# A weight sum moved from VectorE to an accumulating transfer, in four pairs of a feed-forward stage

## The chip, the cores and the metric

The kernel runs on one core of one Trainium2 chip. The metric is the device time of one execution in microseconds (us), as the median of several runs. A core has TensorE for matrix products (PE in the profile; its weight loads are PEld), VectorE (DVE), ScalarE (ACT), GpSimd (POOL) and SyncE (SP). In this kernel SP and POOL do hardly anything but issue transfers. Each engine works through its own queue in order, and waits on semaphores for the others.

## The reference

Two layers work on 512 rows of 1024 numbers in float32: an attention or mLSTM mixer, a cross-attention to a memory of 256 rows, and a feed-forward part with a short causal convolution. Only the last is touched:

```python
def conv_ffn(xn, w_up, conv_w, conv_b, w_down):
    h = causal_depthwise_conv(xn @ w_up, conv_w) + conv_b
    g, u = jnp.split(h, 2, axis=-1)
    return (jax.nn.gelu(g) * u) @ w_down
```

`w_up` is 1024 x 5632 and `w_down` 2816 x 1024.

## The kernel before

Everything is kept transposed: channels on the 128 partitions, the 512 rows along the free axis. The 5632 columns of `w_up` are handled as 22 pairs of 128-wide blocks; pair p holds block p of the half g and block p of the half u. Float32 accuracy comes from splitting each operand into a high and a low part in a faster format (`wh` and `wl`, `xh` and `xl`) and making three matrix products of them: lines L291, L292, L293 in `mm3`. The high part is a cast on ScalarE (L1747, or L285 and L1554 elsewhere), the low part a difference on VectorE (L282).

Pair 0 is done plainly (`plain`). Pairs 1 to 21 go through `seven`, a Strassen-Winograd product: the 2 x 2 blocks (two halves of the weights' rows, g and u; two halves of the input, two halves of the 512 rows) are multiplied with seven products instead of eight. That takes sums of the weights ahead of it, which for each pair are made anew:

- S1 (tile `sa`, 1024 wide): one load on SP, and one accumulating transfer on POOL which adds the other block to it on the way (`onto`, L1732).
- S2 (tile `sb`, 512 wide): the right half of S1 plus the left half of the block A1 (tile `raw`), on VectorE, L1753.
- S4: S2 plus the right half of A1, in place in `sb`, on VectorE, L1759.
- each of S1, S2, S4, A1 and a piece of the other block (`ra`) is then split into high and low.

The products are p1 to p7 in the code. p1 and p2 fill one accumulator (X), p6, p7 and p4 a second (Y), p5 and p3 a third (R). Between them ScalarE copies a state of Y or R away: L1786 (`seed`, Y starts as minus X after p1), L1790 (`kept`: `u5` after p5 from R, `u2` after p6 from Y), and L1793 on VectorE subtracts these. So p6 waits for L1786, p7 for `u2`, p3 for `u5`, and p4 for the L1793 that reads Y. L1816 scales the result by the norm, and `tail` makes the convolution (L1669 on ScalarE, four taps L1676 on VectorE), the gelu (L1684), the product with u (L1686) and its split (`ah`, L1690).

The order of work on each engine is not the order in the code. `add`, `load`, `onto` and `pe` only record tasks for a planner (`Sched`), each with an engine, an assumed duration, what it depends on, a due time, and the buffers it takes and gives back. The planner goes through the tasks engine by engine, always taking the one which could start first, on equal starts the one with the earlier due time; from that follow the queues. A task that is added, removed or given other durations can thus move others. Buffers: `raw` and `sa` have three, `sb` and `ra` two. A buffer of `sb` is taken at S2's making and given back after S4 is split.

Of the kernel before, what the change touches and what calls it, by code (L numbers as in the profile page):

```python
# [65 lines left out]
class Plan:  # L66
# [11 lines left out]
    def add(self, fn, dur=0.0, deps=(), prio=None, take=(), free=(), chain=(), pre=(), after=0.0, order=(), load=(), st=None):  # L78
        it = Item(fn, dur, [d for d in deps if d is not None], len(self.items) if prio is None else prio, take, free, chain, pre, after, order, load, st)
        it.n = len(self.items)  # L80
        self.items.append(it)
        return it
# [154 lines left out]
class Builder:  # L237
# [1269 lines left out]
    def ffn_steps(self, layer, mp):  # L1507
# [5 lines left out]
        add = sc.add  # L1513
        tt = lambda n: 0.055 + 1.06e-3 * n
# [17 lines left out]
        def raw_tile(st, tag):  # L1532
            pool, n, bufs = RAWS[tag]
            st[tag] = self.til(pool, tag, (P, n), bufs=bufs)
            return st[tag]

        def load(st, tag, src, cols, at, dur=0.0017):
            def fn():
                to = raw_tile(st, tag)[:, :cols]
                nc.sync.dma_start(to.rearrange("p (a b) -> p a b", a=2) if len(src.shape) == 3 else to, src)  # L1540

            return add("SP", dur * cols, fn, (), at, [(tag, st)], (), 4.0)

        def parts(st, off=0):
            st["wh"], st["wl"] = self.parts(off)
# [177 lines left out]
        def seven(p, fill):  # L1723
            st, sa, sb, r2, f1, f3, s2, s4, a22 = ({} for _ in range(9))
            at = clock[0]
            A1, A2 = t["up"][layer, p], t["up"][layer, 22 + p]
# [4 lines left out]
            def onto(out, src, cols, deps, due):  # L1731
                return add("POOL", 0.0029 * cols, lambda: nc.gpsimd.dma_start(out(), src(), accum_op=ALU.add), deps, due, (), (), 6.0)  # L1732
# [3 lines left out]
            b1 = load(sa, "sa", up2[p][:, :, :512], 1024, at - 20.0 - soon, 0.0 if soon else 0.0017)  # L1736
            b1 = onto(lambda: sa["sa"][:], lambda: A2, 1024, [b1], at - 16.0 - soon)
            l2 = load(r2, "raw", A1, 1024, at - 12.0)
# [5 lines left out]
            def split(s, cols, deps, due, alloc, take, raw, free=()):  # L1744
                def hi():
                    alloc()
                    nc.scalar.copy(s["wh"][:, :cols], raw())  # L1747

                h = add("ACT", act(cols), hi, deps, due - 3.0, take)
                return add("DVE", tt(cols), lambda: self.sub(s["wl"][:, :cols], raw(), s["wh"][:, :cols]), [h], due - 2.0, (), free)  # L1750
# [1 line left out]
            def s2_():  # L1752
                tt_(out=raw_tile(sb, "sb")[:], in0=sa["sa"][:, 512:], in1=r2["raw"][:, :512], op=ALU.add)  # L1753

            b2 = add("DVE", tt(512), s2_, [b1, l2], at - 5.0, [("sb", sb)])
            w3 = split(f3, 1024, [l2], at, lambda: parts(f3, OFF), [("h", f3)], lambda: r2["raw"][:])
            w2 = split(s2, 512, [b2], at, lambda: small(s2, "s2"), [("s2", s2)], SB)
            w1 = split(f1, 1024, [b1], at + 1.0, lambda: parts(f1, OFF), [("h", f1)], lambda: sa["sa"][:])
# [537 lines left out]
```

## Time and profile before

| | us |
|---|---|
| median of 3 runs (1458.19 to 1459.31) | 1459.03 |
| the profiled execution | 1458.72 |
| its span, first to last instruction | 1456.9 |
| first sum L1753 in layer 0 / in layer 1 | 405.4 / 1108.7 |

The feed-forward stage of layer 0 begins near 406 us and that of layer 1 near 1109 us. In the profile's rows a name like `acc<-xh,wh` is output and inputs by the program's tile names; the first number is the start in us from the span's start, the second the duration, and brackets hold the idle time of that engine ahead of the row and whoever ended it. A duration includes the pipeline's fill, so on a busy engine the distance of two starts is the better price. PE's ends are modelled.

### The profile page before, as it was taken

To read this page: it belongs to the slowest core of one execution; us is meant where nothing else is said; L and a number is where in the kernel's file an instruction comes from. 1 tells how busy PE (TensorE), PEld (TensorE's weight loads), DVE (VectorE), ACT (ScalarE), POOL (GpSimd) and SP (SyncE) were. 2 spreads that over 40 slices of the span, in tenths; PEclk is the share of its full clock that TensorE was granted. 3 is DMA by queue.
4 is the path that set the end of the run, shared out by engine and by line. 5 is a ranking of instruction groups with operands and counts; after the bars stand their busy time and mean duration, and the time that the engine had idled before them with its cause. 6 is when DMAs were issued, how large, how long until landed. Compare 5 with 4: busy or idle time off the path is not lost.

```text
span 1456.9 us, 24068 instructions
## 1 busy us (share of the span) xinstructions
PE 1440.6 (99%) x9019; PEld 1277.7 (88%) x9019; DVE 1225.9 (84%) x2224; ACT 985.5 (68%) x1775; POOL 72.9 (5%) x116
## 2 busy tenths in 40 slices
PE   9999999999999999999999999999999999999998
PEld 7888787998899999999888888889988999999987
DVE  7789987867899988889669988887779998888974
ACT  7689665655677777777547665566566777777764
POOL 0001120000000000000000100000000000000000
PEclk9999999999999999999999999999999999999999
DMA  5222436652246656662233332656413666656322
GB/s 200 87 74 73 118 122 195 169 179 87 94 122 169 183 158 157 155 160 77 84 101 108 111 109 65 204 142 189 131 49 117 162 178 173 154 157 160 104 67 78
DMA packets 70628, 190.24 MB, mean 131 GB/s; under 512 B 7520, under 2 KB 7520, under 8 KB 70512
## 3 DMA queue, kind: packets, MB, share of 16 engines
q1 hardware_dynamic: 62304, 161.38, 35.0%
q0 software_dynamic: 7200, 26.22, 10.6%
q8 instruction: 70, 1.15, 0.3%
q10 hardware_dynamic: 1008, 1.12, 0.2%
q14 instruction: 46, 0.38, 0.1%
HBM read 186.56 MB, written 2.13 MB: 130 GB/s over the span
## 4 chain that ended last, share of the span: by engine, by line
PE 82%; DVE 10%; ACT 4%; issue 2%; DMA 2%; SPq 0%; POOL 0%; ACTq 0%; DVEq 0%; POOLq 0%
PE acc L291 15%; PE acc L292 14%; PE acc L293 14%; PE w L293 6%; PE w L291 6%; PE w L292 6%; PE s L293 3%; PE s L291 3%; PE s L292 3%; PE acc L352 2%; PE acc L354 2%; PE acc L353 2%; DVE wl L282 2%; DMA sa<-in_xq_dram 1%; DVE x L771 1%
## 5 line engine op out<-in xcount | busy, mean ns | idle before, releaser
L282 DVE TENSOR_TENSOR wl<-raw,wh 128x1024 fp32r<-128x1024 f32 (+3 forms) x181 | 213.9, 1182 | 41.2 <-ACT wh L285 32.4
L291 PE MATMUL acc<-xh,wh 128*128 128x256 f32 (+1 forms) x624 | 206.8, 331 | 0.2 <-ACT v L1917 0.2
L293 PE MATMUL acc<-xh,wl 128*128 128x256 f32 (+1 forms) x624 | 205.6, 329 | 0.1
L292 PE MATMUL acc<-xl,wh 128*128 128x256 f32 (+1 forms) x624 | 205.5, 329 | 0.0
L285 ACT CAST wh<-raw 128x1024 fp32r<-128x1024 f32 (+1 forms) x123 | 126.6, 1034 | 84.3 <-PE acc L292 42.9
L1676 DVE SCALAR_TENSOR_TENSOR c<-hs,vec,c 128x512 f32<-128x512 f32 x176 | 130.4, 749 | 16.0 <-ACT c L1669 14.0
L291 PEld LDWEIGHTS acc<-xh,wh 128*128 128x128 f32 x624 | 117.2, 188 | 12.1 <-ACT v L1917 0.6
L293 PEld LDWEIGHTS acc<-xh,wl 128*128 128x128 f32 x624 | 117.2, 188 | 12.0 <-DVE wl L282 0.5
L292 PEld LDWEIGHTS acc<-xl,wh 128*128 128x128 f32 x624 | 117.2, 188 | 11.5
L293 PE MATMUL w<-ah,wl 128*128 128x512 f32 x304 | 119.1, 392 | 0.0
L292 PE MATMUL w<-al,wh 128*128 128x512 f32 x304 | 118.6, 390 | 0.0
L291 PE MATMUL w<-ah,wh 128*128 128x512 f32 x304 | 118.5, 390 | 0.0
L282 DVE TENSOR_TENSOR wl<-sa,wh 128x1024 fp32r<-128x1024 f32 x52 | 63.6, 1222 | 17.0 <-ACT wh L1747 15.6
L1669 ACT ACTIVATE c<-hs,vec 128x512 f32<-128x512 f32 x88 | 71.2, 816 | 9.6 <-DVE hs L1816 8.2
L1747 ACT CAST wh<-sa 128x1024 fp32r<-128x1024 f32 x42 | 44.0, 1049 | 35.5 <-PE w L292 30.5
L293 PEld LDWEIGHTS w<-ah,wl 128*128 128x128 f32 x304 | 57.1, 188 | 12.1
L291 PEld LDWEIGHTS w<-ah,wh 128*128 128x128 f32 x304 | 57.1, 188 | 10.1 <-ACT w L1584 0.2
L292 PEld LDWEIGHTS w<-al,wh 128*128 128x128 f32 x304 | 57.1, 188 | 9.8
L282 DVE TENSOR_TENSOR s<-sb,s 128x512 fp32r<-128x512 f32 x92 | 63.1, 686 | 2.2 <-ACT s L285 0.3
L1554 ACT CAST wh<-dr 128x512 fp32r<-128x512 f32 x64 | 39.7, 621 | 34.2 <-PE w L292 32.2
L1732 POOL DMA_DIRECT2D sa<-in_up_dram x42 | 35.9, 855 | 516.5 <-DVE wl L282 184.5
L291 PE MATMUL acc<-mem,wh 128*128 128x256 f32 (+1 forms) x192 | 61.5, 320 | 0.0
(535 smaller groups left out, 4664.1 us busy)
## 6 DMA issues: line engine op xcount, KB each, us to landing
raw<-in_up_dram SPq DMA_DIRECT2D x46, 512.0 KB, 3.4
sa<-in_up_dram SPq DMA_DIRECT2D x42, 512.0 KB, 4.1
sa<-in_up_dram POOLq DMA_DIRECT2D x42, 512.0 KB, 5.5
dr<-in_down_dram SPq DMA_DIRECT2D x64, 256.0 KB, 2.8
ra<-in_up_dram SPq DMA_DIRECT2D x42, 256.0 KB, 3.1
raw<-in_xk_dram SPq DMA_DIRECT2D x16, 512.0 KB, 3.6
raw<-in_wo_dram SPq DMA_DIRECT2D x16, 512.0 KB, 3.6
raw<-in_xv_dram SPq DMA_DIRECT2D x16, 512.0 KB, 3.4
```

The lines of the kernel that those rows point to most:

```text
L282: self.nc.vector.tensor_tensor(out=lo, in0=v, in1=hi.bitcast(F32), op=ALU.subtract)
L285: self.nc.scalar.copy(hi, v)
L291: mm(out, wh, xh, start=first, stop=False, skip_group_check=parts)
L292: mm(out, wh, xl, start=False, stop=False, skip_group_check=parts)
L293: mm(out, wl, xh, start=False, stop=last, skip_group_check=parts)
L352: mm(ps, xh[k][:, ts], wh[:, ws], start=(k == 0), stop=False)
L353: mm(ps, xh[k][:, ts], wl[:, ws], start=False, stop=False)
L1554: nc.scalar.copy(st["wh"][:, :cols], st[tag][:, :cols])
L1669: nc.scalar.activation(st["c_"][:, j, :], hs()[:, j, 2:514], AF.Identity, scale=self.col("cw", (layer * 3 + 2) * 44 + blk), bias=self.col( ...
L1676: nc.vector.scalar_tensor_tensor(out=c, in0=hs()[:, j, n : n + 512], scalar=w, in1=c, op0=ALU.mult, op1=ALU.add)
L1732: return add("POOL", 0.0029 * cols, lambda: nc.gpsimd.dma_start(out(), src(), accum_op=ALU.add), deps, due, (), (), 6.0)
L1747: nc.scalar.copy(s["wh"][:, :cols], raw())
```

## The change

For pairs 2, 3, 4 and 5 of both layers S2 is no longer made on VectorE. The left half of A1 is loaded a second time from memory, straight into the tile `sb` (SP, 256 KB), and an accumulating transfer on POOL adds the right half of S1, out of `sa`, to it (256 KB, from one place of the on-chip memory to another). The other pairs keep L1753. The buffer of `sb` is now taken when that load is issued. S4 and all splits are the same.

```diff
-            b2 = add("DVE", tt(512), s2_, [b1, l2], at - 5.0, [("sb", sb)])
+            if p in (2, 3, 4, 5):
+                b2 = load(sb, "sb", A1[:, :512], 512, at - 14.0)
+                b2 = onto(lambda: sb["sb"][:], lambda: sa["sa"][:, 512:], 512, [b1, b2], at - 12.0)
+            else:
+                b2 = add("DVE", tt(512), s2_, [b1, l2], at - 5.0, [("sb", sb)])
```

The planner then moves work on all engines within pairs 1 to 8. Behind the edit line numbers are 4 higher in the change (L1759 is L1763, L1793 is L1797, and so on). In the names below the first number belongs to the tile and differs between the programs; `sb_4682`, `sb_4742`, `sb_4948` and `sb_5088` are S2 of pairs 2, 3, 4 and 5 in the change.

First place: VectorE in layer 0, from the end of the normalization (L531) to the L1793 that pair 1's p4 waits for (the row with `acc`). Before:

```order
L531 SCALAR_TENSOR_TENSOR rb_4691<-sqt_4714,sq_4329 128x512
L1713 TENSOR_TENSOR hs_4588<-acc_935_4622,rb_4691 128x512
L282 TENSOR_TENSOR s_962_4789<-sb_4756,s_962_4789 128x512
L1713 TENSOR_TENSOR hs_4588<-acc_941_4664,rb_4691 128x512
L1759 TENSOR_TENSOR sb_4756<-sb_4756,raw_4635 128x512
L1793 TENSOR_TENSOR hs_4587<-s_4741,u_963_4793 128x256
L1676 SCALAR_TENSOR_TENSOR c_4832<-hs_4588,vec,c_4832 128x512
L282 TENSOR_TENSOR wl_4809<-sa_4595,wh_4808 128x1024
L1793 TENSOR_TENSOR hs_4587<-acc_958_4754,u_960_4772 128x256
```

In the change:

```order
L531 SCALAR_TENSOR_TENSOR rb_4693<-sqt_4716,sq_4329 128x512
L1713 TENSOR_TENSOR hs_4588<-acc_935_4622,rb_4693 128x512
L1713 TENSOR_TENSOR hs_4588<-acc_941_4664,rb_4693 128x512
L282 TENSOR_TENSOR s_965_4812<-sb_4682,s_965_4812 128x512
L1676 SCALAR_TENSOR_TENSOR c_4827<-hs_4588,vec,c_4827 128x512
L1763 TENSOR_TENSOR sb_4682<-sb_4682,raw_4635 128x512
L1676 SCALAR_TENSOR_TENSOR c_4827<-hs_4588,vec,c_4827 128x512
L1797 TENSOR_TENSOR hs_4587<-acc_960_4759,u_961_4776 128x256
L282 TENSOR_TENSOR wl_4809<-sa_4595,wh_4808 128x1024
```

The 1024-wide difference of pair 2's S1 and the other L1793 moved behind that L1793, and one tap moved ahead of it.

Second place: ScalarE in layer 0, up to the copy `u<-s` (u5) that pair 3's p3 waits for, and the cast of pair 4's S2. Before:

```order
L1790 COPY u_992_5035<-acc_988_4998 128x256
L1690 CAST ah_5057<-c_4948 128x512
L1747 CAST wh_5054<-sa_4693 128x1024
L1803 COPY hs_4587<-acc_987_4967 128x256
L1669 ACTIVATE c_5098<-hs_4588,vec 128x512
L1790 COPY u_1000_5077<-s_5040 128x256
L1747 CAST s_1005_5113<-sb_5095 128x512
```

In the change:

```order
L1690 CAST ah_5046<-c_4933 128x512
L1794 COPY u_993_5041<-acc_989_5003 128x256
L1747 CAST s_1007_5120<-sb_4948 128x512
L1747 CAST wh_5062<-sa_4695 128x1024
L1807 COPY hs_4587<-acc_988_4973 128x256
L1669 ACTIVATE c_5085<-hs_4588,vec 128x512
L1794 COPY u_1001_5083<-s_5049 128x256
```

The cast out of `sb` moved from behind the copy `u<-s` to four rows ahead of it, and `ah` moved ahead of the copy `u<-acc`.

Third place: the transfers onto `sb` on POOL in layer 0, among those onto `sa` for the pairs behind, in the change (before, only the rows with `sa` stand there):

```order
L1732 DMA sb_4682<-sa_4595 128x512
L1732 DMA sa_4695<-in_up_dram 128x1024
L1732 DMA sb_4742<-sa_4597 128x512
L1732 DMA sa_4890<-in_up_dram 128x1024
L1732 DMA sb_4948<-sa_4695 128x512
L1732 DMA sa_5043<-in_up_dram 128x1024
L1732 DMA sb_5088<-sa_4890 128x512
```

and the loads on SP there, in the change:

```order
L1540 DMA sa_4890<-in_up_dram 128x2x512
L1540 DMA ra_4930<-in_up_dram 128x512
L1540 DMA sb_4948<-in_up_dram 128x512
L1540 DMA raw_5005<-in_up_dram 128x1024
L1540 DMA sa_5043<-in_up_dram 128x2x512
L1540 DMA sb_5088<-in_up_dram 128x512
```

Each transfer onto `sb` stands one row ahead of a transfer onto `sa` for a later pair, and each load into `sb` between loads that stood there before.

## The prediction

> **What bounds the kernel now.** First the page's head: the span and how busy each engine is.
>
> ```profile
> span 1456.9 us, 24068 instructions
> PE 1440.6 (99%) x9019; PEld 1277.7 (88%) x9019; DVE 1225.9 (84%) x2224; ACT 985.5 (68%) x1775; POOL 72.9 (5%) x116
> ```
>
> TensorE (PE) is the bound, POOL is nearly idle. The change acts only at the head of the two feed-forward stages, so I cut these out by windows: pairs 1 to 5 and their tails in layer 0 and in layer 1, and the 25 us after the first. The columns are PE, PEld (weight loads), DVE (VectorE), ACT, POOL, then the granted clock and the DMA share.
>
> ```profile
> 417.00:480.00 63.00, 61.81 (x503) 59.22 (x502) 61.28 (x94) 47.40 (x85) 4.88 (x6) 1.00 0.61 155
> 1120.30:1183.30 63.00, 61.83 (x503) 59.24 (x502) 61.28 (x94) 47.39 (x85) 4.25 (x5) 1.00 0.60 155
> 480.00:505.00 25.00, 25.00 (x175) 23.10 (x175) 25.00 (x42) 18.95 (x34) 1.12 (x2) 1.00 0.68 184
> ```
>
> The two layers run alike to 0.02 us, so one is worked out and doubled. VectorE is full in the first two windows but for 1.72 us, and wholly full in the third, where PE is busy all the same: a full VectorE costs only where PE waits behind it. So the next view is the waits, for the weight loads of 417 to 480 us (the view of 1120 to 1183 us prints the same five rows). Columns: us in total, times, longest.
>
> ```profile
> PEld acc L291 <- ACT acc L1786: 1.1, 2, 0.5
> PEld s L291 <- ACT u L1790: 0.6, 1, 0.6
> PEld acc L291 <- DVE hs L1793: 0.5, 1, 0.5
> PEld s L293 <- DVE wl L282: 0.2, 1, 0.2
> PEld acc L291 <- ACT u L1790: 0.2, 1, 0.2
> ```
>
> These 2.6 us a layer, 5.2 us in all, are all that a lighter VectorE can give back here; the rest is matrix time. Only 0.7 of the 2.6 end on VectorE itself; 1.9 end on ScalarE copies between two products. From the timeline, three of them: PE's rows, and for the second the two ScalarE rows ahead of it.
>
> ```profile
> 427.39 0.19 PEld L291 LDWEIGHTS acc<-kv,a 128*128 128x128 f32 x1 [0.54 <-DVE hs L1793]
> 444.00 0.35 ACT L1790 COPY u<-s 128x256 f32<-128x256 f32 x1
> 444.25 0.62 ACT L1747 CAST s<-sb 128x512 fp32r<-128x512 f32 x1
> 444.40 0.19 PEld L291 LDWEIGHTS s<-xh,s 128*128 128x128 f32 x1 [0.60 <-ACT u L1790]
> 449.53 0.19 PEld L291 LDWEIGHTS acc<-kv,s 128*128 128x128 f32 x1 [0.52 <-ACT acc L1786]
> ```
>
> The copy that starts at 444.00 releases PE 0.40 us after its start.
>
> **What is removed.** Four sums (L1753) a layer, those of pairs 2 to 5. Their price is their spacing on a full VectorE, read from this timeline of DVE:
>
> ```profile
> L1753 DVE TENSOR_TENSOR sb<-sa,raw x42: 680/689/694, 405.4 to 1367.8; 128x512 f32<-128x512 f32 x42
> 426.92 0.42 DVE L1793 TENSOR_TENSOR hs<-acc,u 128x256 f32<-128x256 f32 x1
> 427.25 0.74 DVE L1676 SCALAR_TENSOR_TENSOR c<-hs,vec,c 128x512 f32<-128x512 f32 x1
> 427.91 0.69 DVE L282 TENSOR_TENSOR s<-sb,s 128x512 fp32r<-128x512 f32 x1
> 428.51 0.75 DVE L1676 SCALAR_TENSOR_TENSOR c<-hs,vec,c 128x512 f32<-128x512 f32 x1
> 429.18 1.22 DVE L282 TENSOR_TENSOR wl<-raw,wh 128x1024 fp32r<-128x1024 f32 x1
> 430.31 0.75 DVE L1676 SCALAR_TENSOR_TENSOR c<-hs,vec,c 128x512 f32<-128x512 f32 x1
> ```
>
> Starts differ by 0.60 us for a 512-wide sum or difference (427.91 to 428.51), 0.66 for a tap of L1676, 1.13 for a 1024-wide one (L1816 taken alike), 0.33 for L1793. So 4 x 0.60 = 2.4 us of VectorE time go per layer, 4.8 us in all. That is less than the 5.2 us of waits, but it comes back only through them.
>
> **What is added.** Per pair one more load of 256 KB on SP, and one accumulating transfer of 256 KB on POOL. The nearest rows:
>
> ```profile
> sa<-in_up_dram SPq DMA_DIRECT2D x42, 512.0 KB, 4.1
> dr<-in_down_dram SPq DMA_DIRECT2D x64, 256.0 KB, 2.8
> ra<-in_up_dram SPq DMA_DIRECT2D x42, 256.0 KB, 3.1
> L1732 POOL DMA_DIRECT2D sa<-in_up_dram x42: 844/857/883, 277.0 to 1356.3; - x42
> DMA to landing us min/median/max: 5.2/5.5/8.0
> 427.03 0.38 SPq L1540 DMA_DIRECT2D sa<-in_up_dram  x1
> 431.75 0.85 POOL L1732 DMA_DIRECT2D sa<-in_up_dram  x1 [11.95 <-DMA sa<-in_up_dram]
> ```
>
> The load is priced at 3.1 us, and POOL takes it up some 0.6 us after landing (427.03 + 4.1 = 431.13, taken up at 431.75). An accumulating transfer out of SBUF stands nowhere in the trace. Its bounds: 8.0 us above, the slowest landing of the 512 KB ones, and 2.8 us below, a plain 256 KB load. I take 4.0, nearer the lower end: the 5.5 of twice the bytes, less part of its moving time. The issues themselves cost nothing: 8 x 0.86 us on POOL, 8 x 0.38 us on SP, both with idle time between transfers. The Trainium skill's page DMA: Bandwidth & Descriptors (section on the anatomy of one DMA on the software path) gives about 2.0 us plus the bytes at 436 GB/s, so by estimate 2.6 us here and 3.2 us for 512 KB. By it S2 would be there 1.4 us sooner than below and the charge for its slip, 0.8 us over both layers, would fall away. The trace's 5.5 us for 512 KB stands well above the page's 3.2, so the measurement decides.
>
> Nothing queued behind the new waits suffers. On SP the load for pair 4 waits for the last reader of pair 2's buffer, the difference of S4 on VectorE; behind it stands a raw load which waits for an L1759 (L1763 in the change) that comes later on VectorE anyway. On POOL the next pair's transfer onto sa comes later than its predecessor by construction of the order. What can suffer is ScalarE, whose cast of S2 waits in line for the landing.
>
> **What moves.** With four sums gone VectorE, ScalarE and PE all get a new order, and I walk through the places by the spacings above. PE's rows are the first product of pair 1 and three later matmuls; DVE's are the two waits in the normalization's tail:
>
> ```profile
> 417.36 0.28 PE L291 MATMUL acc<-xh,wh 128*128 128x256 f32 x1
> 443.38 0.28 PE L293 MATMUL acc<-kv,wl 128*128 128x256 f32 x1
> 443.72 0.28 PE L293 MATMUL acc<-kv,wl 128*128 128x256 f32 x1
> 418.40 1.23 DVE L282 TENSOR_TENSOR wl<-raw,wh 128x1024 fp32r<-128x1024 f32 x1 [0.95 <-ACT wh L1747]
> 420.93 0.69 DVE L519 TENSOR_TENSOR sqt<-sqt,rb 128x512 f32<-128x512 f32 x1 [0.70 <-ACT sqt L528]
> ```
>
> Three matmuls take 0.34 us, so a product of twelve takes 1.36. Clock times of the changed kernel are estimates on this profile's clock.
>
> Wait at 427.39 (fourth product of pair 1, on L1793). The normalization's L525 no longer stands behind the 1024-wide difference of 418.40, so the second wait of 0.70 goes: L519 starts at 420.23, and after it and L531 (0.69 each) the first L1713 at 421.6. From there stand ahead of that L1793: two L1713, a difference, a tap, L1759, a tap, 4 x 0.60 + 2 x 0.66 = 3.7 us, so it starts near 425.4 (two steps wait 0.05 on ScalarE) instead of 426.92 and releases PE some 0.4 later, 425.8. The product is now the seventh instead of the eighth, due at 417.36 + 6 x 1.36 = 425.5. The wait: 0.2 (allowing 0.1 of reading) instead of 0.54.
>
> New small waits: p6 of pair 2 on L1786, which now stands behind the table load and two casts, 0.2; p7 of pair 2 on the copy u, now behind the cast ah, 0.25. Both are my reading of the order and may be 0 or 0.5.
>
> Wait at 444.40 (p3 of pair 3, on the copy u). ScalarE's rows there before:
>
> ```profile
> 439.95 0.37 ACT L1790 COPY u<-acc 128x256 f32<-128x256 f32 x1 [0.47 <-PE acc L293]
> 441.47 0.62 ACT L1690 CAST ah<-c 128x512 fp32r<-128x512 f32 x1 [1.14 <-DVE c L1686]
> 442.00 1.05 ACT L1747 CAST wh<-sa 128x1024 fp32r<-128x1024 f32 x1
> 442.95 0.36 ACT L1803 COPY hs<-acc 128x256 f32<-128x256 f32 x1
> 443.28 0.82 ACT L1669 ACTIVATE c<-hs,vec 128x512 f32<-128x512 f32 x1
> ```
>
> The cast ah waits 1.14 us for VectorE. Two sums ahead of L1686 are gone (pairs 2 and 3), 1.2 us, and the earlier tail adds a little, so I put ah at 440.0 (441.47 - 1.2 - 0.3). Behind it now come the copy u of pair 3 (0.35), the cast of pair 4's S2 (0.52), and only then wh, hs, c and the copy that PE waits for (0.95 + 0.33 + 0.72, by the rows): the S2 cast at 440.8, the copy at 443.4, PE released at 443.8 instead of 444.40, no wait. That holds only if S2 of pair 4 is there. Its buffer is pair 2's; on VectorE there stand behind the L1793 of 425.4, by the order, 0.33 + 1.13 + 0.33 + 0.66 + 1.13 + 0.66 + 1.13 + 2 x 0.60, so the last reader starts at 432.0 and ends at 432.7. Load 3.1, take-up 0.6, transfer 4.0: S2 is there at 440.4, 0.4 us ahead of its cast. With the DMA share at 0.61 in this window a slip is likely, and I charge 0.4 us.
>
> Wait at 449.53: gone, since p4 of pair 3 now stands between the two products around the seed L1786. The other L1786 wait (0.5, pair 5) goes too, as three products now stand between the two around it. Instead p3 of pair 4 waits about 0.4 on its copy u, and p4 of pair 4 some 0.1. The last two rows of 0.2 each stay.
>
> Sum per layer: 0.2 + 0.2 + 0.25 + 0.4 + 0 + 0.4 + 0.1 + 0.2 + 0.2 = 1.95 instead of 2.6, so 0.65 us less, 1.3 us for both. The profiled execution took 1458.72 us, its span 1456.9 and 1.8 around it; the median of the three runs shown is 1459.03, 0.3 more. 1458.72 - 1.3 = **1457.4 us**.
>
> **The rivals.** (1) VectorE's time comes off whole: 1458.72 - 4.8 = 1453.9. For it: VectorE is full for over 80 us on end, and every copy on ScalarE follows something of it. Against: 1.9 of the 2.6 us end on ScalarE, and PE loses nothing from 480 to 505 with VectorE full.
>
> (2) S2 comes late, and ScalarE stands: the transfer of pair 4 takes 8.0 us, as the slowest did, and lands at 444.4. ScalarE waits from 440.8, 3.6 us, and behind the cast stand the difference of the same S2, the copy that p3 of pair 3 needs, and the next casts; PE follows one for one. Less the 0.4 charged that is 3.2 us a layer: 1457.4 + 6.4 = 1463.8. It makes the kernel slower by over 2.9 us from 4.2 us above the forecast on, 2.1 a layer and the 0.4: from a wait of 2.5 us, a transfer of 6.9. For it: no slack at this one place. Against: half the bytes, and a median of 5.5 for the whole.
>
> (3) The order's turns of PE, ScalarE and PE cost what they did: 1458.7.
>
> (4) The software queue starves: POOL cannot prepare a transfer while VectorE works, and each of the added ones slips by VectorE's longest operation, 1.22 us: pair 4's S2 then costs 1.2 a layer, 1457.4 + 2.4 = 1459.8. Against it: the 42 issues took 844 to 883 ns each beside a full VectorE. In the Trainium skill this is SBUF — State Buffer, the section on the two separate sides: a GpSimd-issued DMA waits for its descriptors while VectorE holds the shared port pair. By that rule the time would be this rival's; the spread of 39 ns does not agree with it.
>
> **How the numbers follow.** A measurement of this kernel tells about 0.2%, 2.9 us, from no change. Forecast 0.45, (1) 0.25, (2) 0.18, (3) 0.08, (4) 0.04. Faster by over 0.2% is (1) and the upper edge of the forecast, 0.05: 0.30. Slower is (2): 0.18. The rest, 0.52, is within. The forecast's own range is 1455.7 to 1459, with the two small waits at 0 or 0.5 and the charge at 0 or 0.8. The range given leaves out the full price of (1) and the upper end of (2), at which 0.15 lie: 1454.0 to 1463.0.
>
> **What would show it.** Right: L1753 34 times instead of 42; the PEld waits of a layer's window near 1.9 us, no L1786 wait of 0.5, the L1793 wait near 0.2; landings of sb<-sa near 4 us. Wrong upward: a row ACT s L1747 <- DMA sb in ScalarE's waits of over 2 us. Wrong downward: PEld waits under 1 us a layer.

## The result and the profile after

The changed kernel takes 1468.35 us (median of 6 runs, 1466.56 to 1469.92) against 1459.32 us for the kernel before on the same chip (6 runs): a ratio of 1.0064, with an interval of 1.0054 to 1.0073. It is slower by 0.64%; the prediction said 1457.4 us, in a range up to 1463.0. The profiled execution took 1466.93 us, 8.2 more than the one of before and 9.5 more than the forecast.

The head of the page, and then the same two windows as in the prediction (columns: length, PE, weight loads, VectorE, ScalarE, POOL, granted clock, DMA share, GB/s).

```profile
span 1465.2 us, 24086 instructions
PE 1443.2 (99%) x9019; PEld 1282.1 (88%) x9019; DVE 1224.3 (84%) x2216; ACT 984.6 (67%) x1775; POOL 80.5 (5%) x124
417.00:480.00 63.00, 58.54 (x466) 56.75 (x465) 57.50 (x86) 43.90 (x79) 6.87 (x8) 0.97 0.67 165
1120.30:1183.30 63.00, 58.48 (x456) 56.27 (x455) 56.37 (x85) 43.00 (x76) 6.87 (x8) 0.97 0.69 174
```

VectorE has the 8 instructions less and POOL the 8 more that the change promised. But TensorE gets through 466 matmuls in the first window instead of 503: 37 fewer, 4.2 us at the 0.113 us that one takes (in the second it is 456 instead of 503). It stands for 4.46 us of the window (63.00 less 58.54) instead of 1.19, and the granted clock is 0.97 instead of 1.00. The waits of the weight loads from 417 to 480 us, and below them the one wait of ScalarE on a DMA in each layer (the first from 417:480, the second from 1120.3:1183.3):

```profile
PEld s L291 <- ACT u L1794: 4.1, 1, 4.1
PEld acc L291 <- DVE hs L1797: 0.5, 1, 0.5
PEld s L293 <- DVE s L282: 0.4, 1, 0.4
PEld acc L291 <- ACT u L1794: 0.2, 1, 0.2
...
ACT s L1747 <- DMA sb<-sa: 4.0, 1, 4.0
...
ACT s L1747 <- DMA sb<-sa: 4.3, 1, 4.3
```

The two waits on the seed (1.1 us) are gone, as forecast, and the small ones that are left make 1.1 us; one wait of 4.1 us came. It is the place that the prediction named: the product p3 of pair 3, behind the cast of pair 4's S2. The timeline there, ScalarE's rows and then TensorE's two around the gap:

```profile
440.00 0.36 ACT L1794 COPY u<-acc 128x256 f32<-128x256 f32 x1
444.38 0.62 ACT L1747 CAST s<-sb 128x512 fp32r<-128x512 f32 x1 [4.01 <-DMA sb<-sa]
446.83 0.36 ACT L1794 COPY u<-s 128x256 f32<-128x256 f32 x1
...
443.03 0.28 PE L293 MATMUL acc<-kv,wl 128*128 128x256 f32 x1
447.24 0.38 PE L291 MATMUL s<-xh,s 128*128 128x256 f32 x1 [3.94 <-ACT u L1794]
```

ScalarE was ready for the cast at 440.4, stood till 444.38, and the copy that TensorE needed, four instructions further down the same queue, came out at 446.83.

Why was S2 late? SP's rows and POOL's rows around it, then the landing times: of the transfer that makes S1 of pair 5 (issued at 430.81), of the load for S2 of pair 4 (431.89), and of its accumulating transfer (439.27).

```profile
431.29 0.33 SPq L1540 DMA_DIRECT2D ra<-in_up_dram  x1
431.89 0.33 SPq L1540 DMA_DIRECT2D sb<-in_up_dram  x1
...
430.81 0.84 POOL L1732 DMA_DIRECT2D sa<-in_up_dram  x1 [10.91 <-DVE c L1686]
439.27 0.86 POOL L1732 DMA_DIRECT2D sb<-sa  x1 [7.61 <-DVE s L282]
...
sa<-in_up_dram POOLq DMA_DIRECT2D x1, 512.0 KB, 7.4
...
DMA to landing us min/median/max: 6.7/6.7/6.7
...
sb<-sa POOLq DMA_DIRECT2D x1, 256.0 KB, 5.1
```

The load landed 6.7 us after its issue, at 438.6, POOL took the transfer up 0.7 later, and that took 5.1: 12.5 us from issue to landing, where the prediction had 7.7. (The label of the POOL row names a difference on VectorE that ended near by, at 438.84. It is not the releaser to believe: the row waits for the load too, and the kernel below in which the load lands earlier moves POOL's row with it.) What the DMA engines did meanwhile, in windows of 2 us, and how fast TensorE ran behind the gap:

```profile
434.00:436.00 2.00, 2.00 (x20) 2.00 (x19) 2.00 (x4) 2.00 (x4) 0.00 (x0) 1.00 0.98 190
436.00:438.00 2.00, 2.00 (x20) 2.00 (x19) 2.00 (x4) 1.26 (x4) 0.00 (x0) 1.00 1.02 281
438.00:440.00 2.00, 2.00 (x20) 2.00 (x20) 2.00 (x4) 1.32 (x3) 0.73 (x1) 1.00 1.03 407
440.00:442.00 2.00, 2.00 (x20) 2.00 (x19) 2.00 (x4) 0.37 (x2) 0.28 (x2) 1.00 1.00 286
442.00:444.00 2.00, 1.31 (x12) 1.11 (x10) 0.92 (x1) 0.00 (x0) 0.69 (x2) 1.00 1.03 220
...
448.00:450.00 2.00, 2.00 (x13) 2.00 (x13) 2.00 (x5) 1.37 (x2) 0.00 (x0) 0.59 0.17 30
450.00:452.00 2.00, 2.00 (x12) 2.00 (x12) 2.00 (x3) 0.11 (x1) 0.00 (x0) 0.56 0.00 0
452.00:454.00 2.00, 2.00 (x20) 2.00 (x19) 0.75 (x2) 1.49 (x4) 0.00 (x0) 1.00 0.91 275
```

From 434 to 444 us the DMA engines are full in every window, and in the first of them they move only 190 GB/s. The mean share of the 63 us (0.67) shows nothing of that. Behind the gap TensorE issues 25 matmuls in 4 us instead of 40, at a granted clock of 0.59 and 0.56. Two questions were open: is the load late because of the S1 transfer that left 1.1 us ahead of it, and how much of the loss is the clock?

### The profile page after: what moved, and what is told of

It reads as the page before. It is cut to its first block, busy times and chain, and to the rows that moved or that the text cites. A ratio compares the mean times of both kernels' runs of the same rounds, so it can differ in the third digit from the quotient of the medians.

```text
span 1465.2 us, 24086 instructions
## 1 busy us (share of the span) xinstructions
PE 1443.2 (99%) x9019; PEld 1282.1 (88%) x9019; DVE 1224.3 (84%) x2216; ACT 984.6 (67%) x1775; POOL 80.5 (5%) x124
## 3 DMA queue, kind: packets, MB, share of 16 engines
q8 instruction: 70, 1.15, 0.3%
## 4 chain that ended last, share of the span: by engine, by line
PE 82%; DVE 10%; ACT 4%; issue 2%; DMA 1%; POOL 0%; SPq 0%; ACTq 0%; POOLq 0%; DVEq 0%
PE acc L291 15%; PE acc L292 14%; PE acc L293 14%; PE w L291 6%; PE w L293 6%; PE w L292 6%; PE s L291 3%; PE s L293 3%; PE s L292 3%; PE acc L352 2%; PE acc L354 2%; PE acc L353 2%; DVE wl L282 2%; DVE c L1676 1%; DMA sb<-sa 1%
## 5 line engine op out<-in xcount | busy, mean ns | idle before, releaser
L291 PE MATMUL s<-xh,s 128*128 128x256 f32 x200 | 56.7, 283 | 8.8 <-ACT u L1794 8.1
L1732 POOL DMA_DIRECT2D sa<-in_up_dram x42 | 35.9, 855 | 499.4 <-DVE hs L1820 134.0
```

Source lines behind the costliest of these rows:

```text
L291: mm(out, wh, xh, start=first, stop=False, skip_group_check=parts)
```

## Experiments

Line numbers in the rows shift by one or two where an edit adds lines; L1732 is always the accumulating transfer, L1540 the load.

### Which pairs carry the loss

**Pairs 2 and 3 only.**

```
-            if p in (2, 3, 4, 5):
+            if p in (2, 3):
```

> The new way for pairs 2 and 3 only; pairs 4 and 5 sum on VectorE as before. Theory A (the loss sits in one place: S2 of pair 4 lands late, ScalarE waits for it in line, TensorE stands 4.1 us and then runs 3.4 us at half clock, 5.8 us a layer): the place is gone, 1456.5 to 1459.5 us, no ScalarE wait on DMA sb over 1 us, granted clock 0.999. Theory B (each added load and transfer costs a little everywhere, about 1.1 us a pair): half of the loss stays, 1463 us.

Measured: 1459.05 us against 1458.63 before, ratio 1.0002 (0.9993 to 1.0011). No wait on DMA sb in that window, clock 0.999. The loss is not spread evenly over the pairs; theory B falls. No gain shows either.

**Pair 4 only.**

```
-            if p in (2, 3, 4, 5):
+            if p in (4,):
```

> The new way for pair 4 only. Theory A: the late landing is there again, ScalarE wait on DMA sb of 2.5 to 4.5 us a layer and half clock after it if TensorE stands for over 3 us: 1463 to 1468 us. Theory B: a quarter of the loss, 1461 us, with no wait over 1 us.

Measured: 1458.56 us, ratio 0.9999 (0.999 to 1.0008). Theory A missed: with pair 4 alone no cast waits for a landing in layer 0. Its rows of SP and POOL there say why:

```profile
429.16 0.33 SPq L1540 DMA_DIRECT2D sb<-in_up_dram  x1
...
432.46 0.85 POOL L1732 DMA_DIRECT2D sa<-in_up_dram  x1 [12.53 <-DMA sa<-in_up_dram]
433.17 1.04 POOL L1732 DMA_DIRECT2D sb<-sa  x1
...
DMA to landing us min/median/max: 3.4/3.4/3.4
...
sb<-sa POOLq DMA_DIRECT2D x1, 256.0 KB, 7.2
```

In this kernel's order pair 2's buffer comes free earlier. The load leaves 3.3 us ahead of the S1 transfer and lands after 3.4 us (the first landing row); now it is the transfer that runs beside S1 of pair 5, and it takes 7.2 (the last row), but with the earlier start it is there at 440.4. In layer 1 the same transfer takes 8.6, and the cast waits 0.8 us. So the place on ScalarE does not decide alone; it seems to matter on which side of S1's transfer the load falls. From here on this is theory A2.

**Pairs 2, 3 and 5.**

```
-            if p in (2, 3, 4, 5):
+            if p in (2, 3, 5):
```

> The new way for pairs 2, 3 and 5. Pair 5's load waits for pair 3's buffer as pair 4's waits for pair 2's, and on POOL S1 of pair 6 stands ahead of it. Theory A2: if its load leaves within 2 us behind that S1 transfer it lands after 6 us or more, and ScalarE waits 1 to 3 us on S2 of pair 5, 1460 to 1465 us; if it leaves well ahead, 1457.5 to 1459.5. Rival (pair 4 is special for its place on ScalarE alone): 1457.5 to 1459.5 whatever the load does.

Measured: 1458.20 us against 1458.40, ratio 0.9997 (0.9988 to 1.0006), no wait on DMA sb. Pair 5's load leaves at 439.27 and S1 of pair 6 only at 443.20, so both readings expected this, and it tells them apart no further. It shows that three of the four pairs can be changed without a loss. TensorE's row in the first window is looked at below.

### What makes the load late

**S1 of pair 5 without its transfer.** Pair 5's S1 is then half a sum; every other instruction keeps its place in the order of its engine.

```
-            b1 = onto(lambda: sa["sa"][:], lambda: A2, 1024, [b1], at - 16.0 - soon)
+            if p != 5:
+                b1 = onto(lambda: sa["sa"][:], lambda: A2, 1024, [b1], at - 16.0 - soon)
```

> The change, every instruction in its order, but the accumulating transfer that makes S1 of pair 5 (512 KB, taken up at 430.81 us, 1.1 us ahead of the load for S2 of pair 4) is left out, so pair 5's S1 is only half a sum. Theory A2 (the load lands after 6.7 us because that transfer holds the DMA engines): the load lands 3.1 to 4.5 us after its issue, POOL takes S2 up at 435.5 to 437, it lands by 442, ScalarE waits under 1.5 us, no half clock: 1457.5 to 1461 us. Rival (the load is slow because of the loads on its own queue, or because VectorE keeps the transfers from starting): it still takes over 6 us, 1466 to 1468 us.

Measured: 1459.19 us against 1458.40, ratio 1.0004 (0.9996 to 1.0013). SP's row, its landing, POOL's row, its landing, and ScalarE's wait:

```profile
431.79 0.33 SPq L1540 DMA_DIRECT2D sb<-in_up_dram  x1
...
DMA to landing us min/median/max: 2.9/2.9/2.9
...
435.30 0.85 POOL L1732 DMA_DIRECT2D sb<-sa  x1 [16.46 <-DVE wl L282]
...
sb<-sa POOLq DMA_DIRECT2D x1, 256.0 KB, 6.2
...
ACT s L1748 <- DMA sb<-sa: 1.2, 1, 1.2
```

The same load from the same instant lands after 2.9 us instead of 6.7, and POOL takes it up at 435.30 instead of 439.27. That is 3.8 and 4.0 us, and the wait of 4.0 us falls to 1.2: the transfer itself still takes 6.2, beside loads of 512 KB onto raw and onto sa (issued at 433.71 and 434.85). In layer 1 the load falls from 6.6 to 2.9 as well. This settles the cause of the late load, and that it carries nearly the whole loss: 0.60 of the 0.64%. The order of ScalarE's and VectorE's work is the change's throughout the stage of layer 0, and the load onto ra, 0.6 us ahead of it on SP's own queue, is still there, so neither is the cause.

**The transfer onto S2 left out, its load kept.** S2 then lacks the half of S1.

```
-                b2 = onto(lambda: sb["sb"][:], lambda: sa["sa"][:, 512:], 512, [b1, b2], at - 12.0)
```

> All four pairs as in the change, but the accumulating transfer onto S2 is left out (S2 then holds the half of the up weights that was loaded, without S1's half); the added load stays and VectorE's sum stays away. Theory A: S2 is there when its cast comes, since the load alone took 6.7 us from 431.9; the walk of the prediction holds, 1456.5 to 1459 us. Rival on the size of the gain (VectorE's 4.8 us come back whole): 1453.9. Theory B: the loads are as guilty as the transfers, 1463.

Measured: 1456.53 us against 1458.63, ratio 0.9985 (0.9976 to 0.9993): 2.1 us less. The load of pair 4 still took 6.5 us. The window of 417 to 480 us and the waits of its weight loads; below them the same window of the kernel with pairs 2, 3 and 5, and of the one further down that writes S4 into raw:

```profile
417.00:480.00 63.00, 62.72 (x510) 61.00 (x509) 62.10 (x96) 48.55 (x88) 5.13 (x6) 1.00 0.65 168
...
PEld acc L291 <- DVE hs L1796: 0.4, 1, 0.4
PEld acc L291 <- ACT u L1793: 0.2, 1, 0.2
...
417.00:480.00 63.00, 62.72 (x506) 60.94 (x506) 62.44 (x96) 48.76 (x88) 6.89 (x8) 1.00 0.68 174
...
417.00:480.00 63.00, 62.04 (x509) 60.54 (x508) 61.92 (x95) 47.71 (x87) 7.57 (x9) 1.00 0.72 185
```

So this is about what taking the sums off VectorE is worth where nothing is late. The weight loads wait 0.6 us instead of 2.6, and TensorE's own idling falls from 1.19 to 0.28: of 2.0 us less waiting, 0.9 shows there, near half of the 2.1 for two layers. But it is no rule. With pairs 2, 3 and 5 the idling is 0.28 too and the time is that of before (0.9997); with S4 in raw it is 0.96 and the gain 2.1 us again. With differences this small, the idling in one window does not foretell the time.

### What the half clock costs

**36 and 27 idle matmuls in the gap.** They stand ahead of the product that waits, and write a PSUM bank that nobody reads.

```
+            def third():
+                if p == 3:
+                    ps = self.bank("w")
+                    for k in range(36):
+                        nc.tensor.matmul(ps[:, :256], th[k % 4][:, :P], th[k % 4][:, 256:512], start=True, stop=True)
+                product(s4, 0, *X(1, 1), "R", False)
...
-            p3 = pe(n, lambda: product(s4, 0, *X(1, 1), "R", False), [u5, w4], (), [("s4", s4)])
+            p3 = pe(n, third, [u5, w4], (), [("s4", s4)])
```

> The change, with 36 matmuls of 128x256 into an unused PSUM bank put ahead of the product in which TensorE stands (pair 3, products on S4), 4.1 us of work in a gap of 4.1 to 4.4; nothing reads what they write. Clock theory (the half clock after the gap comes from the idling itself): granted clock 1.00 right behind the place, 1.6 to 1.7 us a layer less, 1465.0 us. Rival (the slow matmuls come from what runs beside them, VectorE and ScalarE catching up): the slow stretch stays, 1468.4 us. If the matmuls only push the product back: over 1468.4.

Measured with 36: 1471.07 us against 1458.63, ratio 1.0084 (1.007 to 1.0098). The clock stays at 1.00, so it is the idling that lowers it; but the time is longer than that of the change: neither 1465.0 nor 1468.4. The 36 pushed the product back: it starts at 449.17, though the copy that it waits for started at 447.83. So a second kernel had 27.

> The change with 27 idle matmuls instead of 36 ahead of the same product (3.1 us of work in the gap of 4.1, so that they delay nothing and leave about 1 us of idling). Backlog theory: the granted clock stays at 1.00, but VectorE and ScalarE are behind by the same wait, and TensorE stands for them a few products later: 1467.5 to 1470 us, new waits of 1 us or more. Clock theory (half speed costs its 1.6 us a layer in full): 1464.5 to 1465.5 us.

Measured: 1468.85 us against 1458.52, ratio 1.0072 (1.0058 to 1.0086), the same as the change's 1.0064 within the intervals. Its windows behind the gap, two rows of TensorE and two of ScalarE, and last the two rows of ScalarE in the change:

```profile
448.00:450.00 2.00, 2.00 (x20) 2.00 (x20) 2.00 (x4) 1.62 (x3) 0.00 (x0) 1.00 0.41 73
450.00:452.00 2.00, 1.86 (x17) 1.66 (x15) 2.00 (x4) 0.62 (x1) 0.00 (x0) 1.00 0.46 121
452.00:454.00 2.00, 0.40 (x3) 0.40 (x4) 2.00 (x4) 1.34 (x4) 0.00 (x0) 1.00 0.65 175
...
447.49 0.38 PE L291 MATMUL s<-xh,s 128*128 128x256 f32 x1 [0.30 <-ACT u L1794]
453.60 0.38 PE L291 MATMUL acc<-kv,s 128*128 128x256 f32 x1 [1.75 <-ACT acc L1790]
...
452.66 0.62 ACT L1690 CAST ah<-c 128x512 fp32r<-128x512 f32 x1 [1.73 <-DVE c L1686]
453.18 0.37 ACT L1790 ACTIVATE acc<-acc 128x256 f32<-128x256 f32 x1
...
451.89 0.37 ACT L1790 ACTIVATE acc<-acc 128x256 f32<-128x256 f32 x1 [2.51 <-PE acc L293]
454.08 0.62 ACT L1690 CAST ah<-c 128x512 fp32r<-128x512 f32 x1
```

The product starts at 447.49, 0.25 later than in the change, so it is hardly delayed. Then TensorE runs at 20 matmuls in 2 us, and near 452 it stands for 1.75 us: for the seed L1790 on ScalarE, which stands behind the cast ah, and that waits for VectorE (2.00 busy in all three windows). This is what the backlog theory expected. But the order behind the gap is another one than in the change. There the seed stands ahead of ah, waits 2.51 us for a product that TensorE makes at half clock, and VectorE has work for only 0.75 of the 2 us from 452 on. So the two kernels differ by more than the clock, and the new wait may come from the new order. Shown is that the idling lowers the clock, and that this kernel gained nothing from keeping it up. What the half clock costs in the change, between nothing and 1.5 us a layer (15 intervals of 0.21 us instead of 0.11), stays open.

### A buffer that comes free earlier

**Three S2 buffers, and the kernel before with the same.** The memory came from the second ra buffer.

```
-        sc = Sched(raw=3, h=3, s2=1, s4=1, a22=1, sa=3, sb=2, ra=2, hs=2, c=1, dr=2, u2=1, u5=1, act=10, acc=2, y=2, s=2, w=2)
+        sc = Sched(raw=3, h=3, s2=1, s4=1, a22=1, sa=3, sb=3, ra=1, hs=2, c=1, dr=2, u2=1, u5=1, act=10, acc=2, y=2, s=2, w=2)
...
+        ra2 = [self.til(self.kp, "ra") for _ in range(2)]
...
-            st[tag] = self.til(pool, tag, (P, n), bufs=bufs)
+            st[tag] = ra2[0] if tag == "ra" else ra2[1] if st.get("_sb") == 2 else self.til(pool, tag, (P, n), bufs=bufs)
```

> The change with three S2 buffers instead of two (the memory comes from the second buffer of the 256 KB loads onto ra, which now has one), so that the load for S2 of pair 4 need not wait for pair 2's last reader. Theory A2: the load leaves and lands ahead of the traffic at 431 to 440 us, no ScalarE wait on DMA sb over 0.5 us: 1456 to 1458 us. Rival (the added transfers collide with something wherever they stand): 1460 us or more. The single ra buffer could cost by itself; the next kernel tells.

> Control: the kernel before with the same buffers, three for S2 and one for ra. All theories: 1458 to 1460 us, no difference from before over 0.1%. If it is slower, the single ra buffer is the cause and its excess comes off the result with three buffers.

Measured: 1528.09 us for the change (ratio 1.0484, 1.0469 to 1.0498) and 1533.02 for the kernel before (1.0514, 1.0496 to 1.0532). The single ra buffer costs 5% by itself. No wait on DMA sb was left in the window of layer 0, but the 70 us that the kernel lost elsewhere drown the comparison; nothing follows from these two on the size of the gain.

**S4 into raw instead of over S2, in pairs 2 and 3.** Then S2's buffer comes free behind the sum of S4, not behind its difference.

```
-            b4 = add("DVE", tt(512), lambda: tt_(out=SB(), in0=SB(), in1=r2["raw"][:, 512:], op=ALU.add), [w2], at - 1.5)
+            early = p in (2, 3)
+            S4 = (lambda: r2["raw"][:, 512:]) if early else SB
+            b4 = add("DVE", tt(512), lambda: tt_(out=S4(), in0=SB(), in1=r2["raw"][:, 512:], op=ALU.add), [w2, w3 if early else None], at - 1.5, (), [("sb", sb)] if early else ())
...
-            w4 = split(s4, 512, [b4], at + 5.0, lambda: small(s4, "s4"), [("s4", s4)], SB, [("sb", sb)])
+            w4 = split(s4, 512, [b4], at + 5.0, lambda: small(s4, "s4"), [("s4", s4)], S4, [] if early else [("sb", sb)])
...
-            joined([w3, b2, b4], at, [("raw", r2)])
+            joined([w3, b2, w4 if early else b4], at, [("raw", r2)])
```

> The change, and pairs 2 and 3 write S4 into the second half of their A1 tile (raw) instead of over S2, so that their S2 buffers come free behind the sum of S4 (423 to 424 us for pair 2) and not behind its difference (431.9). Theory A2: the load and the transfer for S2 of pair 4 leave ahead of S1 of pair 5, no ScalarE wait on DMA sb over 0.5 us, and the gain of the kernel without the transfers stays: 1455.5 to 1457.5 us. Rival (the added traffic only hits another transfer, S1 of pair 5 or a raw load whose buffer now comes free later): 1459 us or more, with a ScalarE wait on that tile.

> Control: the kernel before, with S4 of pairs 2 and 3 written into raw in the same way. All theories: 1457.5 to 1459.5 us, within 0.1% of before. What it gains or loses comes off the result with the change.

Measured: 1456.45 us against 1458.52, ratio 0.9987 (0.9978 to 0.9996); the kernel before with the same buffers 1458.64, ratio 0.9998 (0.9989 to 1.0006). The load of pair 4's S2 (a row of its group on SP), POOL's rows, the landing of its transfer, and the two waits left in the weight loads of 417 to 480 us:

```profile
L1540 SPq DMA_DIRECT2D sb<-in_up_dram x1: 328/328/328, 424.2 to 424.2; - x1
...
428.01 0.85 POOL L1732 DMA_DIRECT2D sb<-sa  x1 [7.22 <-DVE c L1676]
430.19 0.86 POOL L1732 DMA_DIRECT2D sa<-in_up_dram  x1 [1.33 <-DMA sa<-in_up_dram]
...
sb<-sa POOLq DMA_DIRECT2D x1, 256.0 KB, 5.0
...
PEld s L291 <- ACT u L1796: 0.7, 1, 0.7
PEld acc L291 <- DVE hs L1799: 0.6, 1, 0.6
```

The load leaves at 424.2 instead of 431.89, its transfer now stands ahead of S1's, and no cast waits. The change with this one edit is faster than both kernels, by 0.13% against the one before, and the edit alone does nothing. It is what the lateness hid: 2.1 us (0.6 to 3.2 by the interval), as much as the kernel without the transfers gained. Here all added transfers run, so this confirms the cause without leaving work out; other work moves in the queues too.

## Why the prediction was wrong

**The arrival of pair 4's S2** is the step that failed: "Load 3.1, take-up 0.6, transfer 4.0: S2 is there at 440.4". The buffer came free at 431.86 (predicted 432.7) and ScalarE reached the cast at 440.4 (predicted 440.8), so the walk on VectorE and ScalarE held. But the load took 6.7, the take-up 0.7 and the transfer 5.1: 12.5 us instead of 7.7, so that S2 was there at 444.4, and the cast 4.0 us late. The load's 3.1 was a median over 42 loads in the whole kernel, and this one left 1.1 us behind a 512 KB transfer; without that transfer it took 2.9. The transfer's 4.0 was too low as well: the eight of the change took 5.1 to 7.2, and where the load came in time, 6.2 left a wait of 1.2 us. The S1 transfer stood in the prediction's own rows, on POOL at 431.75, a microsecond ahead of the load's expected 432.7, but only as a price for the take-up: queues were read for what stands behind the new waits, and not for what stands ahead of the new load on the DMA engines that it shares with them. The slip that was charged, 0.4 us from a share of 0.61 over 63 us, was ten times too small.

**Rival (2)** had the mechanism and the place right, and gave it 0.18. Its cause was wrong: it asked for a transfer of 6.9 us or more, but the transfer took 5.1 and the load made the lateness. Its price was too low as well: it had ScalarE wait 3.6 us a layer, and it waited 4.0 and 4.3. On TensorE's own account the first window has 3.3 us more idling (4.46 less 1.19) and 1.5 us of half clock, 4.8 us in all; twice that is near the 9.0 us measured. It says where the time lies, not what would come back without the half clock.

**The half clock** was in no step. The Trainium skill's page TensorE: Matmul & The Clock Gate, in its part on the clock gate, has TensorE fall to half rate after an idle window of about 3.4 us and return after about as long at work. The trace agrees: TensorE stands 3.9 us, then the granted clock is 0.59 and 0.56 over 4 us; no wait of TensorE in the profile before is as long (1.1 us at most). Whether the half clock adds to the loss stays open, as the experiment with idle matmuls changed the order too.

**The gain** of 1.3 us is not what failed. Waits of weight loads were summed one for one, 2.6 to 1.95 us a layer. They went to 1.1 beside the one long wait (0.5, 0.4 and 0.2), better than the forecast. The two kernels with all four pairs and no late S2 gained 2.1 us each; their intervals (0.6 to 3.2 and 1.0 to 3.5 us) hold the forecast's 1.3 and leave out the 4.8 of rival (1), which falls. With 0.13 to 0.15% that is a gain that the runs can only just tell from none. That one microsecond of these waits is one of time is not shown: where the waits fell by 2.0 us in a window, the idling of TensorE fell by 0.9.

**Rival (4)**, transfers that starve behind VectorE, falls: POOL's issues took 0.84 to 1.15 us beside a full VectorE, and the lateness went with a transfer's absence, VectorE being as full. **Rival (3)**, no gain at all, is what the kernels with one to three pairs measured (ratios 0.9997 to 1.0002); for four pairs with no late S2 it falls, by a narrow margin.

## What to carry to other kernels

Price a new transfer from the stretch in which it leaves, not from the median of its group: look for a large accumulating transfer within a few microseconds ahead of it, on any queue, and at the DMA share in windows of 2 us. Where an added load waits for a buffer, ask first whether the buffer can come free earlier; here one other destination for an intermediate result turned a loss of 0.64% into a gain of 0.13%. And expect little of small waits: 2.6 us of weight-load waits a layer stood beside 1.19 us in which TensorE idled, and no kernel here gained over 2.1 us in both layers. Last, look at the order of the queues before reading a test that adds work: the idle matmuls changed it.

## What the hardware showed that was not expected

- A 256 KB load that leaves 1.1 us behind a 512 KB accumulating transfer on another queue lands after 6.7 us (6.6 in layer 1, 6.5 and 6.6 in two other kernels) instead of 2.9. Where it left 1.7 us behind, it took 5.2 (layer 1 with 27 idle matmuls), and 4.4 us behind, 3.1 (S4 in raw).
- An accumulating transfer of 256 KB from one SBUF tile onto another took 5.1 to 7.2 us in the two stretches of the change, not much less than one of 512 KB from DRAM (5.3 to 7.4): half the bytes did not halve it.
- After TensorE had stood 3.9 us the matmuls did not slow at once: from 447.47 they started 0.11 to 0.12 us apart for a microsecond, then 0.21 apart from 448.44 to 451.65.
